# Two hybrid backbone layers on one core: HGRN2's seven levels as running products on VectorE, two heads staggered, and ScalarE's and GpSimd's shares moved at the inverses and the merge

## The chip, the core and the metric

The kernel is one program on one core of a Trainium2 chip. Its engines run their own instruction queues in order: TensorE (PE; its weight loads are listed as PEld), VectorE (DVE), ScalarE (ACT), GpSimd (POOL), and SyncE (SP), which issues the DMAs. They wait for each other on semaphores. The metric is device microseconds (us) of one launch; three runs of the kernel before took 2661.17, 2665.80 and 2667.43 us.

## The reference

Two layers over 256 context and 256 latent tokens of width 1024, in float32. Each layer:

```
h = h + 0.5 * gate * rms_norm(swiglu(modulate(rms_norm(h))))        # half-step FFN, D_FF 2816
p = split(modulate(rms_norm(h)) @ w_in)                              # one wide projection
ya = gated DeltaNet(p[0:6])      # 4 heads, both directions, needs (I + A)^-1 per chunk
yb = latent attention(p[6:9])    # 4 heads
yc = HGRN2(p[9:13])              # 4 heads, both directions
y  = sum_j sigmoid(p[13]_j) * (y_j @ w_branch_j) @ w_out             # the merge
h  = h + gate * rms_norm(y);  then a second half-step FFN
```

HGRN2 has for every head, direction and key channel a decay f(t) = lb + (1 - lb) * sigmoid and a key k(t) = (1 - lb) * sigmoid(-f). A query at i reads a key at j with weight q(i) * k(j) * (product of the decays between them), and a state carries what lies further back:

```
attn = einsum('bhik,bhjk,bhijk->bhij', q, k, exp(gcum_i - gcum_j))   # per channel
s    = s * exp(g_last) + einsum('ck,cv->kv', k * exp(g_last - gcum), v)
```

In the last layer only the latent half of the tokens is needed after the mixers.

## The kernel before, in words

Activations lie transposed, channels on the partitions and 512 tokens in the row. Every weight slab (128x1024, loaded as `raw` by SP) is split into a rounded part `whi` (ACT cast, `slab`, L194) and a remainder `wlo` (L195: DVE, or POOL where `share` says so), and a float32 product is three matmuls `mm3` (L200 to L202). These fill most of PE's time: `fgu` and `fo` in the FFNs, `pj` (projections and gates), `br` and `po` in the merge.

The mixers are generators: `run_gens(main, fill, ratio)` runs a main generator of dependent work and, by the weight that each `yield` returns times the ratio, steps of a fill generator, which issue `pj` and `br` matmuls between. The instructions of all that are then ordered by a scheduler in the compiler, so a queue's order is not the order of the source.

- DeltaNet (`gdn_pre`): the 32 x 32 inverses come from a recursion on DVE, two transposes (`VD`, `VTD`), copies into `V` and `VX`, and then small matmuls `Y` and `O` with copies `Ys`, `V`, `VX`, `Y6s` between. All these copies alternate between ACT and DVE by `cp` (L828). The fill there is `hg_light` and `hg_gates`, whose `hg_logs` makes log decays: three ACT functions, two DVE operations, three more ACT functions, three DVE operations (a scan among them), one on POOL, for each of 8 gates. `ln_tables` requests an ACT table before each.
- HGRN2 (`hg_mix`, one head after the other): tokens are halved in seven levels, b = 64, 32, ... 1. At each, `Z` is a difference of summed logs to a reference token (POOL for the keys, L1215; DVE for the queries, L1216), an exponential of the whole (ACT, L1217), a product with the query (DVE, L1219), and then matmuls `hps` of keys and queries (L1160, L1228), merged into the tile `hC` by `copy_predicated` (L1240). `qd` is the scaled query (`hqd`, L1178). The levels read only the summed logs `G`, not each other. The fill is `merge` of branch 0 and the gates of branch 1 (`gates_ahead`).
- The merge (`merge`, L1475, L1476): per output tile m, gate times branch product is made on DVE and added into `macc[m]` on POOL. For branch 1 the gates come back by DMA into `sgm`, which has two buffers.
- The output projection: `mh` (ACT, L1567) and `ml` (DVE, L1568) split `macc`; `out_phase` makes eight tiles `po` one after the other, each over eight `mh[k]`, `ml[k]`.

Of the kernel before, what the change touches and what calls it, by code (L numbers as in the profile page):

```python
# [27 lines left out]
RATIO = ((1.2, 0.4, 0.5), (1.1, 0.4, 0.5))  # L28
# [66 lines left out]
def shape_consts():  # L95
# [18 lines left out]
    p["hgm"] = _ct(np.tile(m.transpose(2, 0, 1, 3), (4, 1, 1, 1)).astype(np.int32))  # L114
# [18 lines left out]
class K:  # L133
    def __init__(self, tc, A, es):
# [276 lines left out]
    def ffn_in(self, cols, act, slabs, pre=False):  # L411
# [10 lines left out]
        nc.scalar.activation(sg, ps[0], AF.Silu)  # L422
        a = self.fp.tile([128, n], F32, name="af", tag="af", bufs=2)
# [4 lines left out]
    def ffn(self, l, f, streams=(0, 1), skew=SKEW, ada=(), after=None, start=False):  # L428
# [7 lines left out]
        with ExitStack() as es:  # L436
# [16 lines left out]
            for g, (f0, f1) in enumerate(FG):  # L453
# [28 lines left out]
                def out_tile(m, cols, s):  # L482
# [15 lines left out]
    def out_phase(self, tile_fn, slab_fn, streams, full, nsk, gain, pre):  # L498
# [8 lines left out]
        for m in range(NK - nsk):  # L507
            tile_fn(m, full, slab_fn(m))
            for c in streams:
                sq(c, m, m)  # L510
# [5 lines left out]
        def tile(m, c, slab):  # L516
            tile_fn(m, slice(*HALF[c]), slab)
            sq(c, m, n[c])
            n[c] += 1

        self.by_stream(range(NK - nsk, NK), streams, slab_fn, tile, lambda c: self.norms(c, sums[c], gain, pre, c == streams[-1]))

    def by_stream(self, ids, streams, slab_fn, tile_fn, end=None):

        ids, sl = list(ids), {}
        for c in streams:
            for i in ids:
                if i not in sl:
                    sl[i] = slab_fn(i)
                tile_fn(i, c, sl[i])  # L530
# [6 lines left out]
    def load_consts(self):  # L537
# [9 lines left out]
        ld("hgm", [128, 2, 6, 32], I32)  # L547
# [48 lines left out]
        self.dlb = t("dlb")
        nc.vector.tensor_tensor(self.dlb, self.l1m, self.llb, ALU.subtract)
# [24 lines left out]
    def conv_silu(self, l, i, ps, o):  # L622
# [9 lines left out]
        nc.scalar.activation(o, y, AF.Tanh)  # L632
        nc.vector.scalar_tensor_tensor(o, o, 1.0, y, ALU.add, ALU.mult)
# [49 lines left out]
    def gdn_pre(self, l, last, ph, pb):  # L683
# [139 lines left out]
        eng = [nc.scalar.copy, nc.vector.tensor_copy]  # L823
        ei = 0

        def cp(o, i):
            nonlocal ei
            eng[ei % 2](o, i)  # L828
            ei += 1

        for r in range(4):
            rs = slice(32 * r, 32 * r + 32)
            xs = slice(32 * (r % 2), 32 * (r % 2) + 32)
            cp(V[0][rs, :, rs], VD[rs, :, 0:16].rearrange("x b p -> x p b"))
            cp(V[1][rs, :, rs], VTD[rs, :, 16:32].rearrange("x b p -> x p b"))
            src = VTD[rs, :, 0:16] if r < 2 else VD[rs, :, 16:32]
            cp(VX[rs, :, xs], src.rearrange("x b p -> x p b"))
# [10 lines left out]
        with self.behind(pe, nc.scalar):  # L848
# [253 lines left out]
    def hg_gates(self, l, last):  # L1102

        nc = self.nc
        self.hf = [[self.dram.tile([128, 2, T], F32, name=f"h{n}{l}{h}") for n in "GKk"] for h in range(4)]
        for h in range(4):
            for d in range(2):
                u = 4 * d + h
                slab = self.slab(self.A["win"][l, 26 + u], [128, NK, 128], nc.gpsimd if u % 4 < POOL_LO[l][0] else None)
                self.hg_logs(l, last, u, self.proj(l, 26 + u, slice(0, T), slab))  # L1110
                yield 1

    def hg_logs(self, l, last, u, f):
# [21 lines left out]
        G, GK = big("gls", 2), big("glf", 1)  # L1135
        r = slice(None, None, 1 if d == 0 else -1)
        nc.vector.tensor_tensor_scan(G[:, r], self.rst, lf[:, r], 0.0, ALU.mult, ALU.add)
# [529 lines left out]
```

## Time and profile before

| | |
|---|---|
| three runs | 2661.17, 2665.80, 2667.43 us |
| the profiled execution | 2664.67 us, span 2662.9 us |
| busy in the span | PE 2533.2 us (95%), DVE 1794.2 us (67%), ACT 1145.5 us (43%), POOL 389.6 us (15%) |
| chain that ended last | PE 50%, DVE 6%, ACT 3%, POOL 2% |
| matmul records | 17994 |

A float32 matmul that is not split by hand leaves two records, so counts of `hps` in the trace are twice those in the order. "Busy" of PE joins overlapping matmuls; the rest of the span is time in which no matmul ran. PEclk is the clock that TensorE was granted, as a share of 2.4 GHz; 0.5 is 1.2 GHz. DVE's busy time says nothing by itself of what PE waited for: that stands in the waits.

### The profile page before, as it was taken

To read this page: it belongs to the slowest core of one execution; us is meant where nothing else is said; L and a number is where in the kernel's file an instruction comes from. 1 tells how busy PE (TensorE), PEld (TensorE's weight loads), DVE (VectorE), ACT (ScalarE), POOL (GpSimd) and SP (SyncE) were. 2 spreads that over 40 slices of the span, in tenths; PEclk is the share of its full clock that TensorE was granted. 3 is DMA by queue.
4 is the path that set the end of the run, shared out by engine and by line. 5 is a ranking of instruction groups with operands and counts; after the bars stand their busy time and mean duration, and the time that the engine had idled before them with its cause. 6 is when DMAs were issued, how large, how long until landed. Compare 5 with 4: busy or idle time off the path is not lost.

```text
span 2662.9 us, 45271 instructions
## 1 busy us (share of the span) xinstructions
PE 2533.2 (95%) x17994; PEld 2218.4 (83%) x17994; DVE 1794.2 (67%) x3340; ACT 1145.5 (43%) x1851; POOL 389.6 (15%) x328
## 2 busy tenths in 40 slices
PE   7999999999988999999999999999999898898998
PEld 5888898888877777798888988888889798887998
DVE  7778667675777544487565687777678788745554
ACT  3432235456455343363222443222465655554543
POOL 0000012022233121320000200000212134223001
PEclk9999999999999999999999999999999899998999
DMA  7656544234242241446454446555333335434653
GB/s 263 193 186 200 160 124 152 87 100 150 72 139 88 86 128 56 151 158 189 137 158 143 142 145 205 180 174 169 110 121 123 121 120 197 126 115 143 178 185 121
DMA packets 126179, 385.74 MB, mean 145 GB/s; under 512 B 15248, under 2 KB 26000, under 8 KB 125968
## 3 DMA queue, kind: packets, MB, share of 16 engines
q1 hardware_dynamic: 125968, 382.86, 44.9%
q8 instruction: 141, 2.31, 0.4%
q14 instruction: 70, 0.57, 0.1%
HBM read 355.93 MB, written 26.08 MB: 143 GB/s over the span
## 4 chain that ended last, share of the span: by engine, by line
PE 50%; DVE 6%; ACT 3%; issue 2%; POOL 2%; DMA 1%; SPq 0%; POOLq 0%; ACTq 0%; DVEq 0%
PE fgu L200 8%; PE fgu L202 7%; PE fgu L201 7%; PE fo L201 3%; PE fo L202 3%; PE fo L200 3%; PE pj L201 2%; PE pj L200 2%; PE pj L202 2%; DVE wlo L195 1%; ACT whi L194 1%; PE ssum L288 1%; POOL macc L1476 1%; PE po L200 1%; PE po L201 1%
## 5 line engine op out<-in xcount | busy, mean ns | idle before, releaser
L194 ACT CAST whi<-raw 128x1024 fp32r<-128x1024 f32 (+1 forms) x486 | 501.2, 1032 | 961.8 <-issue 307.2
L195 DVE TENSOR_TENSOR wlo<-raw,whi 128x1024 fp32r<-128x1024 f32 (+1 forms) x444 | 543.1, 1224 | 272.1 <-ACT whi L194 264.5
L200 PE MATMUL fgu<-uh,whi 128*128 128x512 f32 (+1 forms) x1504 | 529.6, 354 | 3.6 <-ACT uh L309 2.2
L202 PE MATMUL fgu<-uh,wlo 128*128 128x512 f32 (+1 forms) x1504 | 529.5, 353 | 0.2 <-DVE wlo L195 0.2
L201 PE MATMUL fgu<-ul,whi 128*128 128x512 f32 (+1 forms) x1504 | 529.3, 353 | 0.1
L200 PE MATMUL pj<-uh,whi 128*128 128x512 f32 (+1 forms) x1072 | 380.3, 356 | 5.9 <-ACT uh L309 3.3
L202 PE MATMUL pj<-uh,wlo 128*128 128x512 f32 (+1 forms) x1072 | 375.6, 352 | 1.0 <-POOL wlo L195 1.0
L201 PE MATMUL pj<-ul,whi 128*128 128x512 f32 (+1 forms) x1072 | 376.6, 352 | 0.0
L224 DVE CUSTOM_DVE_ANT_0 junk<-wa,cb,bada 128x1024 f32<-128x1024 f32 x268 | 343.5, 1282 | 12.8 <-DMA wa<-in_ada 8.6
L200 PEld LDWEIGHTS fgu<-uh,whi 128*128 128x128 f32 x1504 | 286.5, 191 | 42.7 <-ACT uh L309 4.6
L202 PEld LDWEIGHTS fgu<-uh,wlo 128*128 128x128 f32 x1504 | 286.2, 191 | 38.5 <-DVE wlo L195 1.0
L201 PEld LDWEIGHTS fgu<-ul,whi 128*128 128x128 f32 x1504 | 286.5, 191 | 38.0 <-DVE ul L310 0.5
L201 PE MATMUL fo<-al,whi 128*128 128x256 f32 (+1 forms) x896 | 291.3, 325 | 0.5 <-DVE al L426 0.4
L202 PE MATMUL fo<-ah,wlo 128*128 128x256 f32 (+1 forms) x896 | 290.4, 325 | 0.0
L200 PE MATMUL fo<-ah,whi 128*128 128x256 f32 (+1 forms) x896 | 290.4, 325 | 0.0
L277 POOL TENSOR_TENSOR sqa<-sqa,sq 128x256 f32<-128x256 f32 x60 | 65.5, 1091 | 1304.3 <-ACT sq L273 1302.6
L200 PEld LDWEIGHTS pj<-uh,whi 128*128 128x128 f32 x1072 | 208.7, 195 | 28.7 <-ACT uh L309 6.7
L202 PEld LDWEIGHTS pj<-uh,wlo 128*128 128x128 f32 x1072 | 208.3, 195 | 23.7 <-POOL wlo L195 1.4
L201 PEld LDWEIGHTS pj<-ul,whi 128*128 128x128 f32 x1072 | 209.2, 195 | 21.3 <-DVE ul L310 0.4
L201 PEld LDWEIGHTS fo<-al,whi 128*128 128x128 f32 x896 | 168.6, 188 | 17.0 <-DVE al L426 1.6
L200 PEld LDWEIGHTS fo<-ah,whi 128*128 128x128 f32 x896 | 168.4, 188 | 15.4
L202 PEld LDWEIGHTS fo<-ah,wlo 128*128 128x128 f32 x896 | 168.3, 188 | 15.3
(382 smaller groups left out, 3802.1 us busy)
## 6 DMA issues: line engine op xcount, KB each, us to landing
raw<-in_fin SPq DMA_DIRECT2D x184, 512.0 KB, 3.6
wa<-in_ada SPq DMA_DIRECT2D x136, 512.0 KB, 4.1
raw<-in_win SPq DMA_DIRECT2D x128, 512.0 KB, 3.5
raw<-in_fout SPq DMA_DIRECT2D x79, 512.0 KB, 3.5
raw<-in_fout SPq DMA_DIRECT2D x32, 384.0 KB, 3.2
raw<-in_wb SPq DMA_DIRECT2D x24, 512.0 KB, 3.5
raw<-in_wo SPq DMA_DIRECT2D x21, 512.0 KB, 3.8
ws<-in_ada SPq DMA_DIRECT2D x8, 512.0 KB, 7.7
```

The source lines that it names most:

```text
L194: nc.scalar.copy(hi, raw)
L195: (eng or nc.vector).tensor_tensor(lo, raw, hi.bitcast(F32), ALU.subtract)
L200: nc.tensor.matmul(out, wh, xh, start=start, stop=False)
L201: nc.tensor.matmul(out, wh, xl, start=False, stop=False)
L202: nc.tensor.matmul(out, wl, xh, start=False, stop=stop)
L224: op = nc.vector.tensor_tensor_reduce(out=self.junk, in0=w, in1=self.cb[:, t], scale=1.0, scalar=self.bada[:, l, i, m:m + 1], op0=ALU.mult ...
L277: eng.tensor_tensor(S["acc"], S["acc"], sq, ALU.add)
L288: nc.tensor.matmul(S["ps"][:, i:i + 1], a[:, i * 128:(i + 1) * 128], self.ones[:, 0:1], start=S["first"], stop=(m == NK - 1 and a is S["pa ...
L1476: nc.gpsimd.tensor_tensor(self.macc[m][:, cols], self.macc[m][:, cols], sg[i], ALU.add)
```

## The change

It has six parts. (1) `hg_gate` stores the decay itself (`F`) and the key as `K` and drops the second half of the log arithmetic. (2) `hg_mix` goes up from b = 1 to 64: at each level the keys `K` and queries `Q` are multiplied in place by the decay products of the blocks of b tokens, and these products (`D`) are multiplied in pairs for the next level, all on DVE; both directions share one set of matmuls for b < 32, for which ACT copies the keys together (`Kc`). POOL does nothing there, and the slabs' remainders in this stage are all on DVE (`share` is set later). (3) `staggered` runs two heads at once, the next one eight steps behind. (4) At the inverses `cp` is DVE alone, and the first twelve copies alternate POOL and DVE. (5) ACT tables are requested only after a function that needs others. (6) In the merge, branch 1 is added on DVE, the gates and tiles yield in half steps (the ratios double), `ml` moves to POOL, and the output projection makes its first three tiles (`lead`) together, k by k.

```diff
-RATIO = ((1.2, 0.4, 0.5), (1.1, 0.4, 0.5))
+RATIO = ((1.2, 0.85, 1.0), (1.1, 0.85, 1.0))
...
     def ln_tables(self):
+        if not self.other_tables:
+            return ExitStack()
+        self.other_tables = False
         p = self.nc.scalar.preload_act_table_set("natural_log_exp_and_others")
...
-        for m in range(NK - nsk):
-            tile_fn(m, full, slab_fn(m))
+        while m < NK - nsk:
+            ms = list(range(m, m + (lead if m == 0 else 1)))
+            tile_fn(ms, full, [slab_fn(i) for i in ms])
...
-        eng = [nc.scalar.copy, nc.vector.tensor_copy]
-        def cp(o, i):
-            eng[ei % 2](o, i)
+        cp = nc.vector.tensor_copy
+        far = iter([nc.gpsimd.tensor_copy, nc.vector.tensor_copy] * 6)
...
-        with self.behind(pe, nc.scalar):
+        with self.behind(pe):
...
-        e2, lf = big("ge", 2), big("glf", 1)
-        nc.scalar.activation(e2, ls, AF.Abs, bias=c1(self.dlb))
-        nc.scalar.activation(e2, e2, AF.Exp, scale=-1.0)
-        nc.scalar.activation(e2, e2, AF.Ln, bias=1.0)
-        nc.vector.tensor_scalar(lf, ls, c1(self.l1m), c1(self.llb), ALU.add, ALU.max)
-        nc.vector.tensor_tensor(lf, lf, e2, ALU.add)
-        nc.vector.tensor_tensor_scan(G[:, r], self.rst, lf[:, r], 0.0, ALU.mult, ALU.add)
-        nc.gpsimd.tensor_tensor(GK, G, lk, ALU.subtract)
-        for o, t in zip(self.hf[u % 4], (G, GK, lk)):
+        nc.scalar.activation(ls, ls, AF.Exp)
+        nc.scalar.activation(lk, lk, AF.Exp)
+        nc.gpsimd.tensor_scalar(ls, ls, c1(self.omc), c1(self.lbc), ALU.mult, ALU.add)
+        for o, t in zip(self.hf[u % 4], (ls, lk)):
...
+            nc.vector.tensor_tensor(Q, Q, ap(F, T + q0, (-T, 2), (1, nq)), ALU.mult)
+            Dc = F
+            for lev, b in enumerate((1, 2, 4, 8, 16, 32, 64)):
+                if b < 32:
+                    ps = self.pst.tile([128, nch, 32], F32, name="hps", tag="pst")
+                    Kc = big("hKc", 3, nq)
+                    nc.scalar.copy(Kc.rearrange("p (n s b) -> p n s b", s=2, b=b), ap(K, q0, (2 * b, nq // (2 * b)), *kb))
+                    pairs([(lambda t: Kc[:, t - q0:t - q0 + 32], lambda t: ap(Q, t, (2 * b, 16 // b), *qb))], ps)
+                    nc.vector.copy_predicated(C, self.hgm[:, 5 - lev].unsqueeze(1).to_broadcast([128, nch, 32]), ps)
...
+                x = ap(K, 0, (2 * b, nb // 2), *kb)
+                w = ap(Dc, 1, (2, nb // 2), (nb - 1, 2), (0, b))
+                nc.vector.tensor_tensor(x, x, w, ALU.mult)
+                x = ap(Q, 0, (2 * b, nq // (2 * b)), *qb)
+                w = ap(Dc, nb + 1 + q0 // b, (2, nq // (2 * b)), (-nb - 1, 2), (0, b))
+                nc.vector.tensor_tensor(x, x, w, ALU.mult)
+                Dn = pool.tile([128, 2, nb // 2], F32, name="hD", tag=f"hD{b}", bufs=2)
+                nc.vector.tensor_tensor(Dn, Dc[:, :, 0::2], Dc[:, :, 1::2], ALU.mult)
+                Dc = Dn
+                yield 1
...
-        for h in range(4):
-            yield from head(h)
+        yield from staggered([head(h) for h in range(4)], 8)
...
-            for lev, b in enumerate((64, 32, 16, 8, 4, 2, 1)):
-                nc.gpsimd.tensor_tensor(zk, ref, gk, ALU.subtract)
-                nc.vector.tensor_tensor(zq, gq, ref, ALU.subtract)
-                nc.scalar.activation(Z, Z, AF.Exp)
-                nc.vector.tensor_tensor(zq, zq, qq, ALU.mult)
-                    for d in range(2):
-                        pairs([(Z[:, d], Z[:, d])], ps[:, d])
...
-                    nc.gpsimd.tensor_tensor(self.macc[m][:, cols], self.macc[m][:, cols], sg[i], ALU.add)
+                    eng = nc.vector if j == 1 else nc.gpsimd
+                    eng.tensor_tensor(self.macc[m][:, cols], self.macc[m][:, cols], sg[i], ALU.add)
...
-        self.share = SHARE[l]
...
         yb = ynew()
+        self.share = SHARE[l]
...
-                    nc.vector.scalar_tensor_tensor(ml[m][:, cs], self.macc[m][:, cs], 0.5, mh[m][:, cs].bitcast(F32),
+                    nc.gpsimd.tensor_tensor(ml[m][:, cs], self.macc[m][:, cs], mh[m][:, cs].bitcast(F32), ALU.subtract)
...
                 for k in range(NK):
-                    self.mm3(ps[:, cs], wh[:, k, :], wl[:, k, :], mh[k][:, cs], ml[k][:, cs], k == 0, k == NK - 1)
+                    for p, (wh, wl) in zip(ps, sl):
+                        self.mm3(p[:, cs], wh[:, k, :], wl[:, k, :], mh[k][:, cs], ml[k][:, cs], k == 0, k == NK - 1)
...
+def staggered(gens, lag):
+    wait, live, n = list(gens), [], lag
+    while wait or live:
+        if wait and n >= lag and len(live) < 2:
+            live.append(wait.pop(0))
+            n = 0
+        for g in list(live):
+            try:
+                yield next(g)
+            except StopIteration:
+                live.remove(g)
+        n += 1
```

Three places show how the instructions move. The first is VectorE in the first head of HGRN2 in layer 0. Before, with `hZ<-hG` the difference for the queries and `hZ<-hZ,hqd` their product, of several levels at once (the last figures are blocks by b):

```order
L1216 TENSOR_TENSOR hZ<-hG 128x2x8x32
L1216 TENSOR_TENSOR hZ<-hG 128x2x16x16
L1219 TENSOR_TENSOR hZ<-hZ,hqd 128x2x4x64
L1216 TENSOR_TENSOR hZ<-hG 128x2x32x8
L1219 TENSOR_TENSOR hZ<-hZ,hqd 128x2x8x32
L1219 TENSOR_TENSOR hZ<-hZ,hqd 128x2x16x16
L1216 TENSOR_TENSOR hZ<-hG 128x2x64x4
```

And now, `hQ` the queries, `hK` the keys, `hD` the block decays, `hC` the merged products of PE:

```order
L1197 COPY_PREDICATED hC<-c_hgm,hps 128x128
L1214 TENSOR_TENSOR hQ<-hQ,hF 128x256x2
L1211 TENSOR_TENSOR hK<-hK,hD 128x128x2x2
L1216 TENSOR_TENSOR hD<-hD 128x256
L1197 COPY_PREDICATED hC<-c_hgm,hps 128x128
L1214 TENSOR_TENSOR hQ<-hQ,hD 128x128x2x2
L1211 TENSOR_TENSOR hK<-hK,hD 128x64x2x4
L1216 TENSOR_TENSOR hD<-hD 128x128
```

Each level now waits for its own matmuls and works on what the level before it left; before, the differences of later levels stood ahead of the products of earlier ones.

The second place is the inverses of layer 1, the copies that the small matmuls `Y` wait for (`Ys`). Before, one half of them was on ScalarE, behind the gates' functions (`ge`) and table loads:

```order
L1132 ACTIVATE ge<-ge 128x512
L1124 ACTIVATE ge<-ge 128x512
L180 ACT_TABLE_LOAD
L1130 ACTIVATE ge<-gls,dlb 128x512
L1122 ACTIVATE ge<-pj 128x512
L1131 ACTIVATE ge<-ge 128x512
L1123 ACTIVATE ge<-ge 128x512
L1132 ACTIVATE ge<-ge 128x512
L828 COPY Ys<-Y 32x512
```

Now all four are on VectorE, after its six copies, one slab remainder and the first gate's two operations:

```order
L827 STREAM_TRANSPOSE VTD<-X 128x1024
L842 COPY V_18762<-VD 32x16x32
L841 COPY VX<-VTD 32x16x32
L843 COPY V_18763<-VTD 32x16x32
L842 COPY V_18762<-VD 32x16x32
L841 COPY VX<-VD 32x16x32
L843 COPY V_18763<-VTD 32x16x32
L201 TENSOR_TENSOR wlo<-raw,whi 128x1024
L1132 SCALAR_TENSOR_TENSOR gls<-pj,ge 128x512
L1133 TENSOR_TENSOR glk<-gls,pj 128x512
L861 COPY Ys<-Y 32x512 x3
```

So `Ys` has changed its queue, and what stands ahead of it there waits for ScalarE only through one gate.

The third place is PE at the start of the output projection of layer 0, after the last `br`. Before, each group of three matmuls takes the next `mh`:

```order
L200 MATMUL po<-mh_10371,whi 128x256
L201 MATMUL po<-ml_10379,whi 128x256
L202 MATMUL po<-mh_10371,wlo 128x256
L200 MATMUL po<-mh_10372,whi 128x256
L201 MATMUL po<-ml_10380,whi 128x256
L202 MATMUL po<-mh_10372,wlo 128x256
```

Now nine take one:

```order
L206 MATMUL po<-mh_9925,whi 128x256
L207 MATMUL po<-ml_9933,whi 128x256
L208 MATMUL po<-mh_9925,wlo 128x256
L206 MATMUL po<-mh_9925,whi 128x256
L207 MATMUL po<-ml_9933,whi 128x256
L208 MATMUL po<-mh_9925,wlo 128x256
L206 MATMUL po<-mh_9925,whi 128x256
L207 MATMUL po<-ml_9933,whi 128x256
L208 MATMUL po<-mh_9925,wlo 128x256
L206 MATMUL po<-mh_9926,whi 128x256
```

PE has three times the work for every `mh` that has arrived, and needs three slabs of the output weight at its first step.

## Rows read from the trace of the kernel before

**Rows 1.** Stretches: us; busy (instructions) of PE, PEld, DVE, ACT, POOL; PEclk, DMA share, GB/s.

```profile
750.00:910.00 160.00, 139.80 (x2270) 113.68 (x2270) 116.25 (x185) 82.75 (x131) 53.97 (x38) 0.95 0.33 110
2210.00:2310.00 100.00, 87.89 (x1428) 80.88 (x1427) 83.22 (x197) 62.84 (x135) 41.18 (x36) 0.97 0.53 174
2080.00:2120.00 40.00, 28.21 (x297) 23.49 (x297) 25.53 (x35) 31.60 (x41) 5.97 (x4) 0.79 0.32 106
1090.00:1120.00 30.00, 23.69 (x135) 21.09 (x134) 13.17 (x20) 11.50 (x22) 10.72 (x7) 0.83 0.53 185
2400.00:2425.00 25.00, 20.91 (x155) 20.10 (x154) 13.27 (x21) 9.35 (x17) 9.36 (x9) 0.93 0.58 186
0.00:2662.90 2662.90, 2533.24 (x17994) 2218.40 (x17994) 1794.17 (x3340) 1145.47 (x1851) 389.58 (x328) 0.98 0.45 145
```

**Rows 2.** PE's waits over the span: us in total, times, longest.

```profile
PE hps L1160 <- DVE hZ L1219: 12.3, 7, 3.0
PE Y L852 <- ACT Ys L828: 9.6, 1, 9.6
```

**Rows 3.** Groups of `hps` matmuls in 750 to 910 us: busy us, mean ns.

```profile
L1160 PE MATMUL hps<-hZ 128*32 128x32 f32 x1280 | 15.5, 204 | 13.3 <-DVE hZ L1219 7.3 <-issue 5.9
```

**Rows 4.** The same stretches, instructions on `hqd` alone: PE, PEld, DVE busy.

```profile
750.00:910.00 160.00, 3.42 (x256) 2.98 (x256) 33.75 (x40) 0.95 0.33 110
2210.00:2310.00 100.00, 1.97 (x128) 1.53 (x128) 21.17 (x40) 0.97 0.53 174
```

**Rows 5.** The same stretches, line 1216 alone: DVE busy.

```profile
750.00:910.00 160.00, 26.88 (x28) 0.95 0.33 110
2210.00:2310.00 100.00, 16.34 (x28) 0.97 0.53 174
```

**Rows 6.** The same stretches, instructions on `hC` alone: DVE, POOL busy.

```profile
750.00:910.00 160.00, 13.52 (x28) 0.72 (x4) 0.95 0.33 110
2210.00:2310.00 100.00, 9.26 (x28) 0.59 (x2) 0.97 0.53 174
```

**Rows 7.** The same stretches, slab remainders of line 195 alone: DVE, POOL busy.

```profile
750.00:910.00 160.00, 14.36 (x11) 12.01 (x6) 0.95 0.33 110
2210.00:2310.00 100.00, 15.04 (x12) 15.44 (x6) 0.97 0.53 174
```

**Rows 8.** Groups of DVE over the span: busy us, mean ns of one.

```profile
L493 DVE TENSOR_TENSOR y<-y,fo 128x512 f32<-128x512 f32 x24 | 16.5, 686 | 30.0 <-PE fo L202 30.0
L493 DVE TENSOR_TENSOR y<-y,fo 128x256 f32<-128x256 f32 x64 | 26.1, 418 | 42.3 <-PE fo L202 42.2
L1185 DVE TENSOR_TENSOR hC<-hps,c_eyeb 128x128 f32<-128x128 f32 x4 | 1.1, 283 | 0.0
L1244 DVE TENSOR_TENSOR hGK<-hG,hGK 128x1024 f32<-128x1024 f32 x8 | 9.7, 1212 | 0.0
```

**Rows 9.** Instructions in order of time around 766 us: start, us.

```profile
764.15 4.60 POOL L1215 TENSOR_TENSOR hZ<-hG,hGK 128x512 f32<-128x512 f32 x3
766.15 1.59 DVE L1219 TENSOR_TENSOR hZ<-hZ,hqd 128x512 f32<-128x512 f32 x1
```

**Rows 10.** Instructions in order of time, 2084 to 2107 us, the inverses of layer 1.

```profile
2084.40 0.59 DVE L828 COPY V<-VD 32x512 f32<-32x512 f32 x1
...
2088.66 1.10 ACT L828 COPY V<-VTD 32x512 f32<-32x512 f32 x1
...
2106.83 0.58 ACT L828 COPY Ys<-Y 32x512 f32<-32x512 f32 x1
```

**Rows 11.** Instructions in order of time, 1098 to 1107 us, the output projection of layer 0.

```profile
1098.43 0.28 PE L200 MATMUL po<-mh,whi 128*128 128x256 f32 x1
1098.55 0.28 PE L201 MATMUL po<-ml,whi 128*128 128x256 f32 x1
...
1104.79 2.11 POOL L1476 TENSOR_TENSOR macc<-macc,sgm 128x512 f32<-128x512 f32 x1 [1.99 <-DVE sgm L1475]
...
1107.40 0.58 PE L200 MATMUL po<-mh,whi 128*128 128x256 f32 x1 [2.84 <-ACT mh L1567]
```

More of the change, by code (lines that the diff above doesn't have):

```diff
@@ L496, in ffn, with out_phase @@
                 self.out_phase(out_tile, oslab, streams, full, skew if last and split else 0, gain if last else None, after)
-    def out_phase(self, tile_fn, slab_fn, streams, full, nsk, gain, pre):
+    def out_phase(self, tile_fn, slab_fn, streams, full, nsk, gain, pre, lead=1):
         sums = {}
@@ L514, in out_phase, with tile, by_stream @@
         n = [NK - nsk] * 2
[L516 to L523, printed above, removed]
+        def tile(ms, c, slabs):
+            tile_fn(ms, slice(*HALF[c]), slabs)
+            for m in ms:
+                sq(c, m, n[c])
+                n[c] += 1
+        self.by_stream(range(NK - nsk, NK), streams, slab_fn, tile, lambda c: self.norms(c, sums[c], gain, pre, c == streams[-1]), lead)
+    def by_stream(self, ids, streams, slab_fn, tile_fn, end=None, lead=0):
         ids, sl = list(ids), {}
         for c in streams:
[L527 to L530, printed above, removed]
+            rest = list(ids)
+            while rest:
+                n = lead if lead and not sl else 1
+                for i in rest[:n]:
+                    if i not in sl:
+                        sl[i] = slab_fn(i)
+                tile_fn(*((rest[:n], c, [sl[i] for i in rest[:n]]) if lead else (rest[0], c, sl[rest[0]])))
+                rest = rest[n:]
             if end is not None:
@@ L1104, in hg_gates @@
         nc = self.nc
-        self.hf = [[self.dram.tile([128, 2, T], F32, name=f"h{n}{l}{h}") for n in "GKk"] for h in range(4)]
+        self.hf = [[self.dram.tile([128, 2, T], F32, name=f"h{n}{l}{h}") for n in "FK"] for h in range(4)]
         for h in range(4):
@@ L1169, in head @@
             nc.sync.dma_start(q, self.hq[h])
-            C2 = pool.tile([128, 2, nch, 32], F32, name="hC", tag="hC", bufs=2)
-            A = at[h] = pool.tile([128, nch, 128], F32, name="hat", tag="hat", bufs=2)
-            pair = lambda tag, bufs, n=T: pool.tile([128, 2, n], F32, name=tag, tag=tag, bufs=bufs)
-            G, GK, k, qd = pair("hG", 2), pair("hGK", 2), pair("hk", 1, nq), pair("hqd", 1, nq)
-            nc.sync.dma_start(k, self.hf[h][2][:, :, qs])
-            nc.sync.dma_start(G, self.hf[h][0])
@@ L1185, in head @@
-            nc.vector.tensor_tensor(C2[:, 0], ps, self.eyeb.unsqueeze(1).to_broadcast([128, nch, 32]), ALU.mult)
+            pairs([(lambda t, d=d: K[:, d, t:t + 32], lambda t, d=d: Q[:, 1 - d, t:t + 32]) for d in range(2)], ps)
+            nc.vector.tensor_tensor(C, ps, self.eyeb.unsqueeze(1).to_broadcast([128, nch, 32]), ALU.mult)
+            nc.vector.tensor_tensor(Q, Q, ap(F, T + q0, (-T, 2), (1, nq)), ALU.mult)
             yield 0.6
-            yield from levels(h, G, GK, qd, C2, A)
-            C = pool.tile([128, nch, 32], F32, name="hCs", tag="hCs", bufs=1)
```

196 lines of the change are left out of this document (85 added, 111 removed).

## The prediction

> **What bounds the kernel now.** I read the stretches first, then PE's waits, then the groups of VectorE, and last the order of time at three stalls. In the last of [rows 1] a matmul runs in 2533.24 of 2662.90 us: PE sets the time, and a change pays only by shortening PE's own work, the 129.7 us in which none runs, or the time at the lower clock (a stretch of w us at PEclk c does the work of c times w). Five stretches concern the change, and the reader takes from each its length less PE's busy time, and its clock. HGRN2 in layer 0 (750 to 910 us): 20.2 us without a matmul, and 0.05 x 160 = 8 us lost to the clock. HGRN2 in layer 1 (2210 to 2310): 12.1 and 3. The inverses of layer 1 (2080 to 2120): 11.8 and 8.4. The output projection of layer 0 (1090 to 1120): 6.3 and 5.1; of layer 1 (2400 to 2425): 4.1 and 1.8. Together 54.5 and 26 us; that is what there is to win beside PE's own work. The waits [rows 2] name the causes: VectorE's query products before `hps`, and one wait of 9.6 us for `Ys`.
>
> **HGRN2, part by part.** PE first. One set of products now serves both directions for b below 32: 16 fewer matmuls a level and head in layer 0, 5 levels, 4 heads, 320, or 640 records. The 1280 records of `hZ` below b = 32 are busy for 15.5 us [rows 3], 0.0121 us each: 7.7 us less in layer 0. Layer 1 has half the tokens: 3.9 us less.
>
> VectorE loses, in layer 0, all on `hqd` (33.8 us: scaling, query products, last product), the differences of line 1216 (26.9), all on `hC` (13.5) and four `hGK` of 1.21 [rows 4 to 6, 8]: 79.0 us. In layer 1 21.2 + 16.3 + 9.3 + 4.8 = 51.6. It gains per level a key product of 512 in either layer, a query product of 512 (layer 1: 256), a product of the decays of 512, 256, 128 and less, and a merge of half the former width. At the undisturbed prices 0.686 (512), 0.418 (256), 0.283 (128; for everything smaller too, an upper bound) and 1.21 us (1024) [rows 8], layer 0 has 28 x 0.686 keys + 28 x 0.686 queries + 4 x (0.686 + 0.418 + 5 x 0.283) decays + 4 x 1.21 + 8 x 0.686 scalings + 24 x 0.283 merges = 19.2 + 19.2 + 10.1 + 4.8 + 5.5 + 6.8 = 65.6 us; layer 1 19.2 + 11.7 + 10.1 + 2.7 + 3.3 + 6.8 = 53.8. The undisturbed price is right because POOL has nothing to do there any more: beside its differences the same query product took 1.59 us [rows 9]. The price of that is that the six remainders on POOL [rows 7] come to VectorE, at 14.36 / 11 = 1.31 and 15.04 / 12 = 1.25 us: 7.8 and 7.5. VectorE's totals become 116.3 - 79.0 + 65.6 + 7.8 = 110.7 us in layer 0 and 83.2 - 51.6 + 53.8 + 7.5 = 92.9 in layer 1.
>
> PE's totals at full clock become 139.8 - 8 - 7.7 = 124.1 and 87.9 - 3 - 3.9 = 81.0 us. So in layer 0 PE stays the bound, with VectorE 13 us below; in layer 1 VectorE becomes it. What stalls PE in layer 0 is that a head's levels came with few matmuls between; now the order puts 7 to 12 fill matmuls between two levels and the next head's start over the tail of the last. Against it stands a new chain: the levels were independent and are now in series, PE, merge (0.28), query product (0.69), and PE again, with key and decay product beside PE's part. One level is about 0.28 + 0.69 + 0.69 + 0.3 = 1.95 us on VectorE, and PE has 0.85 x 12 fill matmuls for it: products of 256 columns start 0.12 us apart [rows 11], those of 512 about 0.24 (an estimate from these), 2.4 us, and its own. That covers it in layer 0 with little to spare, and not in layer 1, where 0.85 x 12 x 0.12 = 1.2 us stands beside 1.7. The idle time that is left in layer 0 no row shows: its ends are 4 (all covered but the start) and 25 us (more than now); I take 12, and 4 us of clock loss. Gain: 8.2 + 7.7 + 4 = **20 us** (ends 5 and 28). In layer 1 the stretch can't be shorter than VectorE's 92.9; I take 95: **5 us** (ends -12 and 7).
>
> **The inverses of layer 1.** `VTD` is there and the first copy of `V` starts at 2084.40 us; now six copies of 0.59, a remainder of 1.25, two gate operations of 0.69 and two copies `Ys` of 0.59 stand in line on VectorE [rows 7, 8, 10]: 2084.4 + 3.5 + 1.25 + 1.4 + 1.2 = 2091.7, where the last `Ys` came at 2107.4. But PE has 4 matmuls instead of 37 ahead of that wait, 33 x 0.24 = 8 us less cover, and so it comes to it not at 2097.8 (2107.4 less 9.6) but near 2089: a stall of 3, and about 2 for the rest. Idle time falls from 11.8 to 5, the clock loss, which comes from the 32 x 32 products too, from 8.4 to 6: **9 us** (ends 3 and 13). What no row shows is a copy of this shape on VectorE beside one on POOL. The nearest is the two-input pair of [rows 9], 0.9 us longer: six times that is 5.4 us, and 3.6 us of the 9 would be left; from below it costs nothing, as beside ACT's copies in the same rows. I take nothing.
>
> Here the Trainium skill has a rule (SBUF — State Buffer, section Who interferes with whom): VectorE with at most one SBUF input, outside its two-port modes, does not contend with GpSimd, while a copy in such a mode is blocked for GpSimd's whole instruction. The 0.59 us for 512 elements [rows 10] is the pace of one element a cycle and not two, so by the rule the 9 us stand; were the copy in that mode, 3.6. No run here yet shows the two side by side.
>
> **The output projection.** In layer 0 the chain is `macc` on POOL (2.11 us beside VectorE), the next gate's DMA into one of two buffers (the 1.99 before it), ACT, PE [rows 11]: about 4 us for each tile, where PE needs 12 x 0.24 = 2.9. `macc` on VectorE takes 0.69 and no POOL, so the ring falls to about 0.69 + 0.69 + 2.0 less overlap, near PE's pace. And three tiles at once give PE 3 x 3 x 7 = 63 products of 0.12, 7.6 us, before it needs the last `mh`, in place of 2.5. `ml` on POOL costs nothing if it keeps up: 16 halves, each below the 2.11 that a full one takes, beside 8 tiles of 2.9. The three slabs must be there at once; if the third is late, that costs up to the 2.9 us that PE takes for one. I take idle 6.3 to 1 and clock 5.1 to 2 in layer 0, and 4.1 to 2.5 and 1.8 to 1 in layer 1, where the products are half as long and the slabs as large: 8.4 + 2.4 = **11 us** (ends 4 and 14).
>
> **The rest.** Fewer ACT functions, table loads and scans in the gates relieve engines that PE doesn't wait for outside the stretches named: 0 (ends -3 and 4). The finer yields move fill, they don't remove any.
>
> Sum: 20 + 5 + 9 + 11 = 45 us. The profiled execution took 2664.67 us, 1.1 below the median of the runs; 2664.7 - 45 = 2619.7, **2620 us**. What a measurement of this kernel can tell from no change is about 0.2%, 5 us.
>
> **The rivals.**
> *VectorE can't be filled.* In layer 1 it was busy 83% of the stretch [rows 1] with PE idle for 12 us. If 83% is what in-order queues allow, HGRN2 takes 92.9 / 0.83 = 112 us in layer 1 and 110.7 / 0.83 = 133 in layer 0: layer 0 keeps its gain, layer 1 loses 12 instead of winning 5, 2637 us. For it speaks that merge, keys, queries and remainders are in one queue with the readouts; against it, that POOL's interference goes. Chance 0.20. The Trainium skill (Perfetto Trace Analysis, section Optimizing Scalar/DVE Operations) says that with a saturated VectorE work may be offloaded to ScalarE or even GpSimd, which is the change's opposite, and adds that the shared port may undo it.
>
> *Slower: the chain of levels.* 56 levels in series, 28 a layer. If a remainder of 1.25 to 1.31 us stands between merge and query product at each, a level takes about 3.5 us in layer 0 against 2.4 of fill, and 3.2 against 1.2 in layer 1: 28 x 1.1 + 28 x 2.0 = 87 us idle instead of 32.3, +54.7; less 11.6 of matmuls, 9 and 11: +23, 2688 us. It decides from (32.3 + 11.6 + 20) / 56 = 1.1 us of wait a level. Against it: there are only 17 and 18 remainders for 28 levels [rows 7]. Chance 0.07.
>
> *All of it.* Stalls in HGRN2 as good as gone, the clock up everywhere, both projections covered: 28 + 7 + 13 + 14 + 2 = 64 us, 2600. Speaking for it: the order leaves PE fill at every level. Chance 0.18.
>
> **Numbers.** The forecast has 0.55. The range 2597 to 2652 leaves out the slower rival and a part of the ends. Faster by over 0.2%: 0.55 + 0.20 + 0.18 less 0.02 for the tail of the second = 0.91; within: 0.03; slower: 0.06.
>
> **What will show it.** In the profile after: no POOL line in HGRN2 but small ones; `hps` with 960 records fewer; key and query products at 0.69 and 0.42 us; PE's idle time in layer 0's HGRN2 near 12 us and VectorE above 90% busy in layer 1's; the wait of `Y` for `Ys` at 2 to 5 us and on VectorE; no wait of `po` for `mh` above 1.5 us in layer 0. The prediction is wrong if the key products take much more than 0.69 us (their inner runs are short), if PE waits over 1 us a level, or if a new wait appears in a stretch not named.

## The result, and the profile after

The changed kernel took 2624.89 us (median of four runs, 2624.00 to 2626.58) beside 2664.69 for the kernel before: ratio 0.9839, 95% interval 0.9826 to 0.9852. The forecast was 2620. The gain is near the forecast, but it doesn't lie where the forecast put it. The profiled execution took 2624.00 us. The first matmul of each kind marks off the stages; their lengths in us, read from the order of time of both traces, against the terms of the sum:

| stage | before | after | measured | forecast |
|---|---|---|---|---|
| gates and inverses, layer 0 (first `pj` to first `QK`) | 286.0 | 291.6 | +5.6 | 0 |
| HGRN2, layer 0 (first `hps` to first `mkn`) | 186.3 | 156.6 | -29.7 | -20 |
| latent attention, layer 0 (`mkn` to `po`) | 148.2 | 151.3 | +3.1 | 0 |
| output projection, layer 0 (`po` to `fgu`) | 61.7 | 51.0 | -10.7 | -8.4 |
| gates and inverses, layer 1 | 259.9 | 257.5 | -2.4 | -9 |
| HGRN2, layer 1 (first `hps` to first `mkn`) | 99.8 | 99.1 | -0.7 | -5 |
| latent attention, layer 1 | 93.6 | 91.9 | -1.7 | 0 |
| output projection, layer 1 | 44.9 | 43.5 | -1.4 | -2.4 |
| all the rest | | | -2.8 | 0 |
| sum | | | -40.7 | -45 |

These are lengths in one execution each. Between the kernels of the experiments, stages whose own code is the same differ by up to 2 us in layer 0, but in layer 1 by up to 4.6 us at the inverses, 2.4 in HGRN2 and 5.2 in the attention. The small differences of layer 1 therefore say little.

Stretches of the changed kernel, with the columns of [rows 1]: the two HGRN2 stages up to the last readout, two stretches at the inverses (the first in layer 0, the second in layer 1), the output projection of layer 0, the span.

```profile
766.00:899.00 133.00, 132.48 (x1666) 106.08 (x1665) 97.06 (x207) 55.27 (x109) 0.00 (x0) 1.00 0.34 112
2182.00:2274.00 92.00, 84.91 (x1101) 77.92 (x1102) 79.70 (x208) 45.91 (x112) 2.39 (x1) 0.96 0.52 169
585.00:600.00 15.00, 5.61 (x40) 5.40 (x39) 13.65 (x9) 4.02 (x5) 12.74 (x8) 0.72 0.28 83
2047.00:2075.00 28.00, 18.72 (x172) 14.63 (x171) 22.26 (x19) 7.04 (x12) 14.75 (x10) 0.70 0.28 86
1074.00:1126.00 52.00, 49.83 (x416) 49.20 (x415) 33.94 (x68) 31.48 (x65) 19.17 (x21) 1.00 0.50 158
0.00:2622.20 2622.20, 2520.09 (x17034) 2205.32 (x17034) 1768.82 (x3352) 1045.75 (x1738) 284.39 (x268) 0.98 0.45 144
```

Layer 0's HGRN2 leaves PE 0.5 us without a matmul, at the full clock; GpSimd does nothing in it. Layer 1's leaves 7 us, with VectorE busy for 87% of it. The third line is new: for 9.4 of 15 us PE stands still, and the clock falls to 0.72. In the kernel before, the same place in layer 0 was

```profile
585.00:600.00 15.00, 13.21 (x112) 13.01 (x112) 6.96 (x12) 11.77 (x15) 4.81 (x2) 1.00 0.28 84
```

Those of PE's waits after that bear on the change (us in total, times, longest), to be set beside [rows 2]:

```profile
PE mpt L1415 <- DVE mp L1411: 10.6, 5, 5.1
PE pbc L675 <- DVE ry L664: 9.4, 1, 9.4
PE pj L208 <- POOL wlo L201: 4.7, 1, 4.7
PE Y L858 <- DVE Ys L861: 4.6, 1, 4.6
PE hps L1204 <- DVE hD L1216: 2.2, 3, 0.9
```

The old waits have shrunk: `hps` from 12.3 us to a few, `Y` from 9.6 to 4.6. No wait of `po` for `mh` is left in layer 0. Three have grown: `pbc` for `ry` (layer 0, 1.8 us before), `pj` for a remainder on GpSimd (layer 1, 1.0 before), and `mpt` for `mp` (4.4 in all before, none above 1.4). Here is the first of them in order of time (start, us), VectorE, then GpSimd, then PE:

```profile
586.50 1.02 DVE L842 COPY V<-VD 32x512 f32<-32x512 f32 x1
587.54 1.48 DVE L841 COPY VX<-VTD 32x512 f32<-32x512 f32 x1
...
593.04 2.75 DVE L843 COPY V<-VTD 32x512 f32<-32x512 f32 x1
595.80 2.22 DVE L664 TENSOR_SCALAR ry<-ry 128x16 f32<-128x16 f32 x1
...
587.08 1.48 POOL L842 COPY V<-VD 32x512 f32<-32x512 f32 x1
...
592.75 5.24 POOL L201 TENSOR_TENSOR wlo<-raw,whi 128x1024 fp32r<-128x1024 f32 x2
592.75 2.58 POOL L201 TENSOR_TENSOR wlo<-raw,whi 128x1024 fp32r<-128x1024 f32 x1
595.28 2.71 POOL L201 TENSOR_TENSOR wlo<-raw,whi 128x1024 fp32r<-128x1024 f32 x1
...
598.08 1.33 PE L675 MATMUL pbc<-ident,ry 128*128 128x128 f32 x5 [9.39 <-DVE ry L664]
```

The copy that took 0.59 us beside ScalarE's [rows 10] takes 1.02 to 1.48 beside GpSimd's copy. Beside a GpSimd remainder it takes 2.75, and a `TENSOR_SCALAR` of 16 elements takes 2.22. The two remainders (listed once together and then one by one) end at 595.33 and 597.99; the copy ends 0.46 us after the first, `ry` 0.03 after the second. `ry` stands behind the copies in VectorE's queue, and PE's `pbc` behind `ry`.

What the prediction said of HGRN2's instructions is there: `hps` has 1632 records for 2592 before, 960 fewer, and the products of keys and queries take 0.68 to 0.72 us for 512 elements and 0.42 for 256 at six of the seven levels. At the first, where the other operand is `hF`, they take 1.14 and 1.15, and 0.62 (groups over the span: busy us, mean ns):

```profile
L1162 PE MATMUL hps<-hQ,hKc 128*32 128x32 f32 x960 | 16.3, 202 | 1.5 <-DVE hQ L1183 1.0 <-DVE hQ L1214 0.4
L1211 DVE TENSOR_TENSOR hK<-hK,hD 128x512 f32<-128x512 f32 x48 | 34.3, 715 | 6.5 <-PE hps L1204 3.8 <-ACT hKc L1195 2.3
L1214 DVE TENSOR_TENSOR hQ<-hQ,hD 128x512 f32<-128x512 f32 x24 | 16.4, 684 | 0.0
L1214 DVE TENSOR_TENSOR hQ<-hQ,hD 128x256 f32<-128x256 f32 x24 | 10.1, 419 | 0.0
L1211 DVE TENSOR_TENSOR hK<-hK,hF 128x512 f32<-128x512 f32 x8 | 9.1, 1137 | 0.0
L1214 DVE TENSOR_TENSOR hQ<-hQ,hF 128x512 f32<-128x512 f32 x4 | 4.6, 1152 | 0.0
```

### The profile page after: what moved, and what is told of

It reads as the page before. It is cut to its first block, busy times and chain, and to the rows that moved or that the text cites. A ratio compares the mean times of both kernels' runs of the same rounds, so it can differ in the third digit from the quotient of the medians.

```text
span 2622.2 us, 43024 instructions
## 1 busy us (share of the span) xinstructions
PE 2520.1 (96%) x17034; PEld 2205.3 (84%) x17034; DVE 1768.8 (67%) x3352; ACT 1045.7 (40%) x1738; POOL 284.4 (11%) x268
## 3 DMA queue, kind: packets, MB, share of 16 engines
q1 hardware_dynamic: 122000, 375.42, 44.9%
## 4 chain that ended last, share of the span: by engine, by line
PE 83%; DVE 9%; ACT 3%; DMA 2%; issue 2%; POOL 1%; SPq 0%; POOLq 0%; ACTq 0%; DVEq 0%
PE fgu L208 11%; PE fgu L206 11%; PE fgu L207 11%; PE pj L206 6%; PE pj L207 6%; PE pj L208 6%; PE fo L207 5%; PE fo L208 5%; PE fo L206 5%; DVE wlo L201 1%; PE pbc L675 1%; PE ssum L295 1%; ACT whi L200 1%; PE br L206 1%; PE br L207 1%
## 5 line engine op out<-in xcount | busy, mean ns | idle before, releaser
L201 DVE TENSOR_TENSOR wlo<-raw,whi 128x1024 fp32r<-128x1024 f32 (+1 forms) x460 | 560.7, 1220 | 266.4 <-ACT whi L200 257.4
```

The lines of the kernel that those rows point to most:

```text
L201: (eng or nc.vector).tensor_tensor(lo, raw, hi.bitcast(F32), ALU.subtract)
```

## The experiments

Each is the changed kernel with one edit, or two that are named. The kernel before ran beside each of the three groups in which they were measured, with medians of 2667 to 2669 us, so ratios are what is compared; that of the changed kernel is 0.9839.

### The new stall at the inverses

**All twelve copies on VectorE.**

```diff
-        far = iter([nc.gpsimd.tensor_copy, nc.vector.tensor_copy] * 6)
+        far = iter([nc.vector.tensor_copy] * 12)
```

> The twelve copies ahead of the inverses, which the changed kernel deals out to GpSimd and VectorE in turn, are all on VectorE; nothing else is changed. Theory 1 (the copies of the two engines hold each other up, and VectorE's queue behind them is late): the copies take 0.55 to 0.7 us each again, the wait of pbc for ry in layer 0 (9.4 us) falls below 3, the stage from the first pj to Y in layer 0 from 213.5 to 203 to 207 us, the wait of Y for Ys in layer 1 to at most 5; in all 2611 to 2618 us. Theory 2 (it is the GpSimd remainders, 5.2 us for two beside ry, whatever the copies do): copies quick, but pbc still waits over 6 us; 2620 to 2626. Theory 3 (VectorE's queue is simply too long there): twelve copies in place of six make it longer, 2626 to 2632.

2623.12 us, ratio 0.9835 (0.9818 to 0.9851): no change. VectorE in order of time, and GpSimd's remainders:

```profile
589.32 0.61 DVE L841 COPY VX<-VTD 32x512 f32<-32x512 f32 x1
589.86 2.74 DVE L842 COPY V<-VD 32x512 f32<-32x512 f32 x1
592.52 2.73 DVE L843 COPY V<-VTD 32x512 f32<-32x512 f32 x1
595.26 0.59 DVE L841 COPY VX<-VD 32x512 f32<-32x512 f32 x1
...
589.57 5.24 POOL L201 TENSOR_TENSOR wlo<-raw,whi 128x1024 fp32r<-128x1024 f32 x2 [14.98 <-ACT whi L200]
```

Ten copies take 0.6 us again, so GpSimd's copies had held them up. Two wait out a remainder each (4.3 us more), and six more copies of 0.6 stand in the queue (3.5 us): the wait of `pbc` stays at 8.9 us. What theory 1 holds of the copies is true, but its time is not; what came is theory 2's, quick copies, a wait above 6 us and 2620 to 2626.

**The six on ScalarE.** `far` alternates `nc.scalar.copy` and `nc.vector.tensor_copy`.

> Of the twelve copies the six that were GpSimd's are ScalarE's, alternating with VectorE; nothing else is changed. Theory 1 (contention of GpSimd and VectorE): VectorE's copies take 0.55 to 0.7 us, ScalarE's about 1.1; the long wait of pbc in layer 0 is gone, stage pj to Y 203 to 207 us; in layer 1 ScalarE is in the middle of the gates' functions, so up to 4 us come back there; 2611 to 2620 us in all. Theory 2 (the GpSimd remainders are the cause): the wait stays above 6 us, 2621 to 2627.

2612.14 us, 0.9793 (0.9776 to 0.9810). The wait of `pbc` is 1.6 us, layer 0's stage from the first `pj` to the first `Y` 202.4 us in place of 213.5. VectorE's copies take 0.58 to 0.63. ScalarE's copies also delay its casts, so that the remainders start behind `ry`, at 592.29: both forms of the hold-up are gone, and this run doesn't part them. In layer 1 the wait of `Y` for `Ys` rises from 4.6 to 9.0, since ScalarE's gate comes later.

**No remainder on GpSimd in this stage**, with all copies on VectorE (the edit above), and in a second kernel with the six on ScalarE:

```diff
-POOL_LO = ((2, 1), (2, 1))
+POOL_LO = ((0, 0), (0, 0))
```

> All twelve copies ahead of the inverses on VectorE, as in e1_far_dve, and the remainders of the gates' and values' weights, of which GpSimd took up to half, on VectorE too: in this stage GpSimd has no tile-sized work left. Theory 2 (what held e1_far_dve back is that two of its copies wait out a GpSimd remainder each, 2.7 us in place of 0.6): no copy above 0.65 us, the wait of pbc for ry in layer 0 below 3 us, stage pj to Y 203 to 207 us in layer 0, in layer 1 VectorE has 7 us of copies ahead of the gate and Ys, so the wait of Y stays 4 to 9; in all 2608 to 2617 us. Theory 3 (VectorE's queue is too long as such): the remainders make it longer, the waits stay or grow, 2622 to 2635.

> The six GpSimd copies on ScalarE, as in e2_far_act, and the remainders of the gates' and values' weights on VectorE. Theory 2 (contention alone is to blame): layer 0 like e2_far_act (pj to Y 202 to 206 us), layer 1's wait of Y for Ys falls from e2_far_act's 9.0 to 6 to 8, because the remainder ahead of Ys takes 1.25 in place of 2.52 us; 2608 to 2613 us. Theory 3 (VectorE's queue as such): five more remainders on it cost more than the contention did, 2615 to 2625.

2607.65 us, 0.9771 (0.9756 to 0.9785), and 2603.05, 0.9758 (0.9741 to 0.9774). No copy takes over 0.65 us, though each remainder has moved onto the queue said to be too long: theory 3 falls, and both kernels are a little faster than theory 2 had them. The wait of `Y` for `Ys` is 3.8 and 3.7, and layer 1's stage, 257.5 us in the changed kernel and 257.3 and 257.4 in the two runs above, falls to 250.4 and 250.3. In these two the scheduler also put `ry` ahead of the copies (at 581.4 in the first, 0.166 us), which by itself would end the wait of `pbc`; the durations of the copies don't depend on that.

### HGRN2

**Heads one after another**, `chain` of the four in place of `staggered`; **less fill** in layer 0; and both.

```diff
-        yield from staggered([head(h) for h in range(4)], 8)
+        yield from chain(*[head(h) for h in range(4)])
```
```diff
-RATIO = ((1.2, 0.85, 1.0), (1.1, 0.85, 1.0))
+RATIO = ((1.2, 0.4, 1.0), (1.1, 0.85, 1.0))
```

> HGRN2's heads run one after another in place of staggered; the levels, products and engines are those of the changed kernel. Theory A (staggering is what fills PE): in layer 0 between the first hps and the last readout PE is without a matmul for 8 to 20 us more (stage 132.4 to 142 to 155), in layer 1 for 8 to 15 more (92.0 to 100 to 107); 2640 to 2660 us. Theory B (the fill between the levels and GpSimd's absence do it, the stagger adds little): both stages within 3 us of the changed kernel's, 2622 to 2630.

> In HGRN2 of layer 0 the fill between two steps is at the kernel before's ratio, 0.4 in place of 0.85; the fill that is not used there runs behind it. Theory A (fill covers the chain of a level): with about half of it, 1.2 us, beside 1.95 us of VectorE's a level PE is idle 0.5 to 0.9 us at each of 28 levels; from the first hps to the first mkn 156.6 becomes 168 to 182 us; 2634 to 2650. Theory B (the second, staggered head is cover enough): within 4 us of 156.6, 2622 to 2629.

> HGRN2's heads one after another and, in layer 0, the kernel before's ratio of fill, both at once; each alone left layer 0's stage as it was. Theory A (either cover is enough, neither is not): from the first hps to the first mkn of layer 0 165 to 182 us in place of 156.6, PE waiting for hQ or hC; with layer 1's 8 us of the serial heads 2644 to 2662. Theory B (without GpSimd's products beside them the levels are short enough for PE's own work and half the fill): within 4 us of 156.6, 2633 to 2640.

Serial: 2635.55 us, 0.9882 (0.9861 to 0.9903). Less fill: 2624.96, 0.9835 (0.9820 to 0.9850). Both: 2637.78, 0.9887 (0.9869 to 0.9906). In layer 0 the first `hps` to the first `mkn` takes 157.7, 157.0 and 159.9 us beside 156.6: neither of the covers that the prediction relied on is needed there, and without both 3.3 us are lost. In layer 1 the stagger is worth 8.0 us (92.0 to 100.0 up to the last readout). Theory A was right for layer 1 alone, and in total the serial heads lie between both theories.

**Key products on GpSimd**, the 56 of line 1211:

```diff
-                nc.vector.tensor_tensor(x, x, w, ALU.mult)
+                nc.gpsimd.tensor_tensor(x, x, w, ALU.mult)
```

> The 56 products of keys and block decays of HGRN2 are on GpSimd in place of VectorE, the rest is the changed kernel. GpSimd's strided 128x512 product took 4.60 / 3 = 1.53 us before. Theory X (GpSimd's tile products hold VectorE up for as long as they run, as its remainders did the copies): layer 1's VectorE has 79.7 - 19.7 + 28 x 1.53 = 103 us of work and waiting, its stage goes from 92.0 to 100 to 112 us; layer 0 has 97 - 19.2 + 43 = 121, which PE's 132 cover, so its stage grows by 0 to 8; 2634 to 2652. Theory O (an overloaded VectorE is relieved): layer 1's stage falls to 74 to 84, as with no key products, layer 0's stays; 2607 to 2617.

2651.48 us, 0.9936 (0.9915 to 0.9958). Layer 0's stage to the last readout goes from 132.4 to 143.9, layer 1's from 92.0 to 99.2. VectorE's busy time in layer 1 doesn't fall (81.7 in 100 us, 79.7 in 92 with the products), though 22.4 us of products have left it: what remains takes longer, the query products 594 ns in place of 419 and the remainders 1508 in place of 1219. That is theory X, a little low on layer 0 and a little high on layer 1. GpSimd's own product is slower than VectorE's too (1393 ns in the mean), and PE waits for it; how much of the loss is that, the run doesn't say.

**Fill's remainders on GpSimd again**, six a layer:

```diff
         self.mt = rs.enter_context(pool(name="mt", bufs=1, side=R))
+        self.share = SHARE[l]
```

> Every third weight remainder of HGRN2's fill is on GpSimd again, some 6 a layer at 2.4 us, in place of VectorE's 1.25; the rest is the changed kernel. Theory X (VectorE stands still while GpSimd does a remainder): layer 1's VectorE gets 79.7 - 7.5 + 14.4 = 86.6 us, its stage goes from 92.0 to 95 to 100, layer 0's stays within 2; 2626 to 2634. Theory O (offloading relieves the engine that sets the stage): layer 1's stage falls by 5 to 7.5, 2617 to 2620.

2635.84 us, 0.9873 (0.9849 to 0.9897); the four runs lie between 2626.9 and 2636.8, and the profile is of the lowest. Both theories missed the place: layer 1's stage to the last readout shortens to 89.2, layer 0's grows from 132.4 to 142.0, in an execution that is only 2.9 us longer as a whole. Three rows from layer 0, VectorE and GpSimd in order of time, show how so few remainders can cost that:

```profile
808.33 0.16 DVE L270 SCALAR_TENSOR_TENSOR rt<-rt,rv 128x4 f32<-128x4 f32 x1
808.52 2.35 POOL L201 TENSOR_TENSOR wlo<-raw,whi 128x1024 fp32r<-128x1024 f32 x1 [28.14 <-DVE rt L270]
808.53 2.35 DVE L271 SCALAR_TENSOR_TENSOR ry<-rt,ry 128x4 f32<-128x4 f32 x1
```

An instruction of four elements, 0.16 us, lasts as long as GpSimd's remainder of 1024, and PE waits 2.1 us for it. In all, PE is without a matmul for 6.7 of the 142 us; the other waits were not followed up. Why layer 1 gains 2.8 us all the same stays open; other kernels with the changed kernel's code there are up to 1.7 us shorter than it.

**No key products in layer 1.**

```diff
-                nc.vector.tensor_tensor(x, x, w, ALU.mult)
+                if l == 0:
+                    nc.vector.tensor_tensor(x, x, w, ALU.mult)
```

> Leaves out the 28 products of keys and block decays of HGRN2 in layer 1 (the keys stay undecayed there); everything else is the changed kernel. Theory V (VectorE's whole work sets layer 1's HGRN2): 28 x 0.69 = 19 us less of it, the stage from the first hps to the last readout falls from 92.0 to 79 to 84 us, where PE's own work stops it; 2612 to 2617 us. Theory C (the chain merge, query product, PE of one level after the other sets it, and the key products lie beside it): the stage within 3 us of 92, 2621 to 2626. In between (85 to 89) both, since the keys stand in the same queue.

2614.78 us, 0.9797 (0.9783 to 0.9812). The stage falls by 20.0 of the 22.4 us that the products take, further than theory V had it (79 to 84), until PE's own work stops it:

```profile
2184.00:2256.00 72.00, 71.12 (x1011) 64.55 (x1011) 57.28 (x176) 40.67 (x103) 0.00 (x0) 1.00 0.55 184
```

Theory V: VectorE sets layer 1's stage. By itself the run doesn't exclude a chain in which the key product stands ahead of the matmuls, since `Kc` is copied from its result. The serial heads speak against that: if a chain of levels set the stage, it should cost far more than 8.0 us to run the heads without overlap. That is argued, not shown. Some 10 of the 20 us come back later, where the fill that wasn't used runs.

### The output projection, and the best version

**One tile at the start**, the last argument of `out_phase` 1 in place of 3.

> The output projection starts with one tile in place of three at once; the rest is the changed kernel. Theory A (the three tiles give PE work while mh arrives): layer 0's projection goes from 51.0 to 56 to 59 us, layer 1's from 43.5 to 45 to 46.5, with po waiting for mh; 2631 to 2636 us. Theory B (the quicker accumulation on VectorE made the difference, mh is there in time anyway): both within 1.5 us, 2624 to 2627.

2627.48 us, 0.9845 (0.9824 to 0.9866): in total no difference from 0.9839. Layer 0's projection takes 53.0 us beside 51.0 and 61.7, layer 1's 43.8 beside 43.5. Three tiles at once are worth 2.0 and 0.3 us; the other 8.7 of layer 0 don't come from them. That they come from `macc` on VectorE was not tried by itself.

**Best.** The six copies on ScalarE, `POOL_LO` zero, and no remainders on GpSimd in the latent attention:

```diff
-SHARE = (3, 3)
+SHARE = (0, 0)
```

> As e8_act_no_pool_lo (the six copies on ScalarE, no remainder of the gates' and values' weights on GpSimd) and MLA's remainders, some 6 a layer on GpSimd, on VectorE too. Theory X (the waits of mpt for mp, 10.4 us, one of 5.1, are VectorE standing still behind a GpSimd remainder of 2.34): they fall to at most 4, MLA's stages (151.3 and 93.7 us) by 3 to 7 and 2 to 6; 2591 to 2600. Theory Q (mp is late by VectorE's own queue): seven more remainders of 1.25 in it make it no better, stages within 2 us, 2601 to 2608.

2599.28 us, 0.9743 (0.9726 to 0.9761), the fastest of all. The wait of `mpt` for `mp` falls to 5.2 us (longest 2.8), not quite theory X's 4. The attention's stages shorten by 3.0 and 5.0 us against the kernel with the first two edits alone; in layer 1 that is within what the stage differs by anyway, and that kernel's ratio of 0.9758 has an interval that overlaps.

## Why the prediction was right or wrong

**Right in total, by two errors against each other**: HGRN2 and projection of layer 0 gave 40.4 us in place of 28.4, everything else together 0.3 in place of 16.4.

**The inverses: the step that failed** is "I take nothing" for a copy on VectorE beside one on GpSimd. VectorE's six copies take 9.4 us in layer 0 and 9.3 in layer 1 in place of 3.5. The alternative in the text, 0.9 us longer each and 5.4 in all, is near that: five take 1.02 to 1.48. Not thought of was that copies so drawn out run on into the time of GpSimd's remainders, where the sixth takes 2.75 and the instruction behind it waits out a remainder too. (In layer 0 the first remainder starts at 592.75; in the kernel before it started at 592.36, when VectorE's copies and `ry` were done.) When the copies are all on VectorE and quick, the remainders come to them: ScalarE, free of copies, makes its casts earlier, and the first remainder starts at 589.57.

In layer 0 this cost 10.3 us up to the first `Y`, of which 4.8 came back behind it, where the prediction saw no term at all: it named the wait of layer 1, and didn't ask who waits behind the same copies in layer 0. The last of its signs of being wrong, a new wait in a stretch not named, is this one. In layer 1 it left 2.4 of the 9 us, near the lower alternative, 3.6, and not the one taken. There VectorE's own remainder behind the copies takes 3.27 us in place of 1.25, and PE waits 4.7 us for a remainder of GpSimd's that stands behind GpSimd's six copies. With copies and remainders both off GpSimd the stage is 9.6 us shorter than before, which is what the 9 had promised; how much of that is VectorE held up, and how much GpSimd itself late, the runs don't part.

The evidence stood in the kernel before, in its latent attention, in order of time:

```profile
1048.92 2.35 POOL L195 TENSOR_TENSOR wlo<-raw,whi 128x1024 fp32r<-128x1024 f32 x1
1049.30 0.17 DVE L1432 RECIPROCAL mmx<-mmx 128x1 f32<-128x1 f32 x1 [0.63 <-ACT mp L1431]
1049.50 1.92 DVE L1433 TENSOR_SCALAR mp<-mp,mmx 128x256 f32<-128x256 f32 x1
1051.47 0.20 PEld L1437 LDWEIGHTS mpt<-ident,mp 128*128 128x128 f32 x2 [1.84 <-DVE mp L1433]
```

The last of VectorE's two takes 0.35 us elsewhere: it has one tensor input, and it ends 0.15 us after GpSimd's remainder. The mean of its group (549 ns for 256 elements, 595 for 512) gave it away. This is also where the prediction misread the rule of the Trainium skill (SBUF — State Buffer, section Who interferes with whom). The page says that copies and scalar operations can enter the modes in which they block against GpSimd, by conditions on their operands; the prediction judged the mode by the pace, one element a cycle. The trace agrees with the page's list and not with that reading: a copy of that pace is held until GpSimd's instruction ends. The part of the rule that two-input operations contend agrees (2.35 us for four elements).

**HGRN2, layer 0: mechanism right, size off.** The idle time that was taken as 12 us, between 4 and 25, is 0.5, and the clock loss of 4 is 0. The reason given, fill between levels and a second head, is not what clears it: both could be removed for 3.3 us. What matters is GpSimd's absence: key products put back on it cost 11.5 us, six remainders 9.6. VectorE at 97 us of 133 has room, and the levels in series then stay ahead of PE. Whether that absence alone would have done, with the old levels on VectorE, was not tried. Of the 29.7 us, 10.9 lie behind the last readout, where less fill is left to run.

**HGRN2, layer 1: the step that failed** is that a stage bound by VectorE would be as long as its work, 95 us for 92.9. Its work was less, 79.7 us in 92.0. The products were priced nearly right, but the working adds up whole instructions, and here most start about 0.08 us before the one ahead of it has ended: the 208 of the stretch add up to 95.1 us and are busy for 79.7. And it filled only 87%. Up to the last readout the stage even grew by 3.9 us; 4.6 came back between there and `mkn`. That is the rival *VectorE can't be filled*, which supposed 83%, in its mechanism; its times, 112 us and 2637, didn't come, as the work was less. In layer 0, where PE sets the stage, the rival is not put to the test. The remedy named beside it, work moved on to GpSimd, is what the Trainium skill (Perfetto Trace Analysis, section Optimizing Scalar/DVE Operations) doubts for the port that the two share, and the runs bear the doubt out: the key products there raised the ratio from 0.9839 to 0.9936. The slower rival, the chain of levels, didn't come.

**The output projection: right**, 12.1 for 11, but the three tiles, which carried half of the argument, gave 2.3. **The rest: not nothing.** Latent attention in layer 0 lost 3.1 us, with a wait of 5.1 us for `mp`, 2.0 of it of the same kind as above:

```profile
966.58 2.34 POOL L201 TENSOR_TENSOR wlo<-raw,whi 128x1024 fp32r<-128x1024 f32 x1
966.71 2.35 DVE L1411 TENSOR_SCALAR mp<-mp,mmx 128x256 f32<-128x256 f32 x1
```

Without the remainders on GpSimd this instruction takes 0.35 us, the wait is 2.8, and the 3 us are back.

## What to carry to other kernels

Before work is put on GpSimd or taken from ScalarE beside VectorE, look in the trace for small VectorE instructions whose duration is that of a GpSimd instruction beside them; a group mean above its shape's price shows them. A move that relieves one engine also brings forward what stood behind it: ask which instructions will now run side by side. Taking GpSimd's remainders and copies from it, though VectorE got the larger part of them, was worth another 25 us here (ratio 0.9839 to 0.9743).

## What the runs showed of the hardware

A GpSimd operation on two SBUF tensors that is under way holds VectorE's copies, `TENSOR_SCALAR`s and operations with two SBUF inputs until it ends, down to a few elements a partition: 0.16 us became 2.35, 0.17 became 2.22, 0.59 became 2.75. Operations with an operand in PSUM (`hst`, `hps`) went on beside GpSimd's key product, in the run that has it there:

```profile
799.61 1.18 POOL L1211 TENSOR_TENSOR hK<-hK,hD 128x512 f32<-128x512 f32 x1 [0.73 <-ACT hKc L1195]
799.73 0.47 DVE L1247 COPY hS<-hst 128x128 f32<-128x128 f32 x2
800.12 0.33 DVE L1249 SCALAR_TENSOR_TENSOR hS<-hS,hD,hst 128x128 f32<-128x128 f32 x1
800.56 0.30 DVE L1197 COPY_PREDICATED hC<-c_hgm,hps 128x128 f32<-128x128 int32 x1
800.77 0.68 DVE L1214 TENSOR_TENSOR hQ<-hQ,hD 128x512 f32<-128x512 f32 x1
```

The first operation with both inputs in SBUF, `hQ`, comes only as GpSimd's ends, so these rows say nothing of it. A reciprocal of one element a partition was not held either (0.17 us at 1049.30 above), nor, in the kernel before, a `TENSOR_SCALAR` of one element (0.15 us, three times beside a GpSimd operation).

It works the other way round too; in these rows the one that starts second is held. In the kernel before, `macc` on GpSimd took 1.26 us by itself and 2.11 where a remainder of VectorE's had started 0.23 us ahead of it ([rows 11] have the second of these rows):

```profile
1104.56 1.22 DVE L195 TENSOR_TENSOR wlo<-raw,whi 128x1024 fp32r<-128x1024 f32 x1
1104.79 2.11 POOL L1476 TENSOR_TENSOR macc<-macc,sgm 128x512 f32<-128x512 f32 x1 [1.99 <-DVE sgm L1475]
```

The second of GpSimd's two remainders beside the copies, 2.71 us in place of 2.40, fits that: it started 0.5 us before the copy that had waited for the first was done.
